# LoRA router: one exponential's row sum from ScalarE's accumulator output

## The chip, the cores and the metric

The kernel runs on one core of one Trainium2 chip. A time is the device time of one execution in microseconds (us). The kernel before took 86.59 us, the median of four runs that lie from 86.5 to 86.7.

## What is computed

A router gives each token a softmax over eight adapters. The reference is

```python
batch, seq, dim = 16, 512, 1024
num_loras = 8
# x: (16, 512, 1024) float32, router_weights: (1024, 8) float32

logits = np.matmul(x, router_weights)
exp_logits = np.exp(logits - np.max(logits, axis=-1, keepdims=True))
return (exp_logits / np.sum(exp_logits, axis=-1, keepdims=True)).astype(np.float32)
```

There are 8192 tokens of 1024 numbers: 32 MiB of x are read, and 8192 x 8 probabilities (256 KB) are written.

## The kernel before

**Tiling.** Token number p * 64 + j lies on partition p in row j, so each of the 128 partitions holds 64 rows (J = 64) of 1024 numbers. Each row j (128 tokens, one per partition) is one unit of work. TensorE transposes its eight 128x128 pieces (KO = 8); five land in the PSUM tile ptv and three in pts. VectorE copies ptv to xTv (L403), ScalarE copies pts to xTs (L355), and TensorE multiplies the eight pieces with the weights w_bf into eight logits per token, in the PSUM tile lg (L269 in the loop, L261 behind it). The loop of TensorE also multiplies a filler tile that is used for nothing.

**Softmax in groups.** For eight rows at a time (G = 8) VectorE takes the row maxima (L423, tile mx) and the differences (L423, tile ex), ScalarE the exponentials (L344, tile ev), and VectorE the sums (L439, ssum), the reciprocals (L443, inv) and the scaling into out_all (L423). These are spread between the copies of later rows.

**The end.** The last four rows (ALONE = 4) are not part of a group. For each, `low_alone(k)` takes the negated row maximum on VectorE (L454, tile low), and `power_alone(k)` the exponential on ScalarE with that maximum as bias (L348), from PSUM into row k of ev3. The last of all, row 63, arrives in three pieces; its transposes are at L315, their copies at L385 (ScalarE) and L460 (VectorE), its multiplication at L329. Then VectorE scales the last group (L423, `scale()`), sums the four rows of ev3 into sum3 (L507), takes four reciprocals into inv3 (L509) and multiplies (L511). In the profile ev and ev3 are both called ev, sum3 is called sum, and inv and inv3 are both called inv.

**Transfers.** GpSimd issues the loads of x with a cast to bf16 (L174, and L187 for the three pieces of row 63); the first four rows come from SyncE's queue. SyncE stores the result in two transfers: all rows but the last twelve (L165), and the last twelve (L167) when scaling and final product are both done.

**Order.** No scheduler moves anything: each engine's instructions stand in the order in which the code writes them, and engines wait for each other by semaphores that are written out. The ones that matter here are s_low (a row maximum is ready, VectorE to ScalarE), s_e3 (an exponential of the last four rows is ready, ScalarE to VectorE and TensorE), s_d (VectorE for itself, between dependent steps) and s_out (rows of the result are ready, VectorE to SyncE). A wait is written in two ways. `dve.wait_ge(s, n)` in front of an instruction is built into that instruction. `dve.wait_ge(s, n).then_inc(s, -n)`, which also counts the semaphore down, is built as an instruction of its own that stands in front; in the loop the waits ahead of L423 (row maxima), L439 and L344 are of this second kind, behind the loop they are of the first.

## Time and profile before

| what | value |
|---|---|
| median of four runs | 86.59 us (86.5 to 86.7) |
| the profiled execution | 86.53 us |
| its span, first to last instruction | 85.1 us |
| granted clock of TensorE, mean | 0.989 |
| HBM read | 33.59 MB, 398 GB/s over the span |
| TensorE busy (matmul) | 62.9 us, 74% |
| VectorE busy | 39.5 us, 46% |
| ScalarE busy | 38.0 us, 45% |
| one L348 exponential (128x8, bias from a tile) | 267 to 274 ns |
| the sum L507, reciprocal L509, product L511 | 186, 179, 192 ns |
| last store (48 KB), issue to landing | 1.5 us |

The table of busy time gives averages over the whole span. The order of the last operations is read from the timeline and from the chain of work that ended last, whose times are in microseconds from the span's start. An operation's row shows when it ran and not its wait; what ended the idle time in front of it stands in brackets behind it, as `[0.20 <-ACT ev L348]`. A name with a q, such as DVEq, is the engine's own sequencer: the engine was idle until its instruction stream got on.

### The profile page before, as it was taken

How to read it: one execution, taken by the hardware profiler on the slowest of the kernel's cores; microseconds unless marked ns; L12 is line 12 of the kernel's file. 1: busy time of each engine (PE TensorE's matmuls, PEld its weight loads, DVE VectorE, ACT ScalarE, POOL GpSimd, SP SyncE). 2: the span in 40 equal slices, each digit the busy share in tenths (PEclk: the TensorE clock that was granted, in tenths of full speed). 3: DMA queues.
4: the chain of work that ended last, by engine and by line, in shares of the span. 5: the costliest groups of instructions: out<-in, count | busy, mean ns of one | idle time of the engine just before them, and what ended most of it. 6: DMA issues, size and time to landing. Idle time of an engine off the chain costs nothing. (4 is left out here: it accounts for less than half of the span.)

```text
span 85.1 us, 2942 instructions
## 1 busy us (share of the span) xinstructions
PE 62.9 (74%) x1094; PEld 51.6 (61%) x1094; DVE 39.5 (46%) x114; ACT 38.0 (45%) x81; POOL 13.5 (16%) x30
## 2 busy tenths in 40 slices
PE   0054859999595977949596895949597799999860
PEld 0042748878484765828474673837476588777650
DVE  0020412685364442835266362736347257665662
ACT  0039683565254352535245262525336246545470
POOL 0489999800000000000000000000000000000000
PEclk9999999999999999999999999999999999999995
DMA  2999999999999999999999999999999999999920
GB/s 58 358 424 308 220 193 235 196 235 196 235 196 235 196 235 196 235 196 235 196 235 196 235 196 235 196 235 196 231 200 206 214 216 212 203 211 205 190 104 23
DMA packets 3904, 18.12 MB, mean 213 GB/s; under 512 B 568, under 2 KB 1080, under 8 KB 2112
## 3 DMA queue, kind: packets, MB, share of 16 engines
q0 software_dynamic: 3312, 15.73, 90.5%
q1 hardware_dynamic: 576, 2.36, 7.2%
q10 hardware_dynamic: 16, 0.03, 0.2%
HBM read 33.59 MB, written 0.26 MB: 398 GB/s over the span
## 5 line engine op out<-in xcount | busy, mean ns | idle before, releaser
L355 ACT COPY xTs<-pts 128x384 bf16<-128x384 bf16 x63 | 30.0, 477 | 37.4 <-PE pts L282 37.0
L403 DVE COPY xTv<-ptv 128x640 bf16<-128x640 bf16 x63 | 30.9, 491 | 32.9 <-PE ptv L282 30.4
L282 PE MATMUL ptv<-identity,x_all 128*128 128x128 bf16 x311 | 28.4, 223 | 13.6 <-PEq L218 12.3
L282 PEld LDWEIGHTS ptv<-identity,x_all 128*128 (+1 forms) x311 | 18.6, 98 | 15.0 <-issue 14.9
L282 PE MATMUL pts<-identity,x_all 128*128 128x128 bf16 x186 | 21.1, 224 | 0.0
L269 PEld LDWEIGHTS lg<-w_bf,xTv 128*128 128x128 bf16 x305 | 15.5, 98 | 7.4 <-issue 0.5
L269 PE MATMUL spare<-filler 128*128 128x512 bf16 x61 | 19.0, 393 | 0.5
L269 PE MATMUL lg<-w_bf,xTv 128*128 128x8 bf16 x305 | 16.6, 167 | 0.0
L282 PEld LDWEIGHTS pts<-identity,x_all 128*128 x186 | 13.5, 100 | 0.0
L269 PE MATMUL lg<-w_bf,xTs 128*128 128x8 bf16 x183 | 13.2, 166 | 0.0
L174 POOL DMA_DIRECT2D x_all<-in_x_dram x20 | 10.8, 605 | 2.8 <-POOLq L151 2.8
L269 PEld LDWEIGHTS lg<-w_bf,xTs 128*128 128x128 bf16 x183 | 8.9, 96 | 0.0
L269 PEld LDWEIGHTS spare<-filler 128*128 128x128 bf16 x61 | 4.3, 99 | 2.5 <-issue 2.5
L276 PE MATMUL lg<-ident,w 8*128 8x8 f32 x8 | 1.0, 250 | 5.3 <-PEq L274 5.3
L276 PEld LDWEIGHTS lg<-ident,w 8*128 8x128 f32 x8 | 0.9, 197 | 5.3 <-issue 5.3
L341 ACT CAST x_all<-x_f 128x1024 bf16<-128x1024 f32 x4 | 4.0, 1044 | 0.0
L423 DVE TENSOR_REDUCE mx<-lg 128x8 f32 x8 | 1.8, 224 | 4.4 <-DVEq L473 3.9
L341 ACT ACT_TABLE_LOAD x1 | 1.3, 1283 | 5.5 <-ACTq L339 5.5
L392 DVE CAST identity<-ident 128x128 bf16<-128x128 f32 x1 | 0.5, 516 | 5.3 <-POOL ident L180 5.3
L344 ACT ACTIVATE ev<-ex 128x64 f32<-128x64 f32 x8 | 2.1, 256 | 1.6 <-DVE ex L423 0.9
L439 DVE TENSOR_REDUCE ssum<-ev 128x8 f32<-128x64 f32 x8 | 1.8, 221 | 0.0
L187 POOL DMA_DIRECT2D x_all<-in_x_dram x3 | 1.7, 690 | 0.0
(41 smaller groups left out, 16.0 us busy)
## 6 DMA issues: line engine op xcount, KB each, us to landing
x_all<-in_x_dram POOLq DMA_DIRECT2D x12, 1024.0 KB, 32.1
x_f<-in_x_dram SPq DMA_DIRECT2D x2, 1024.0 KB, 6.3
x_all<-in_x_dram POOLq DMA_DIRECT2D x3, 512.0 KB, 59.9
x_all<-in_x_dram POOLq DMA_DIRECT2D x5, 256.0 KB, 64.1
out_dram<-out_all SPq DMA_DIRECT2D x1, 208.0 KB, 1.9
x_all<-in_x_dram POOLq DMA_DIRECT2D x1, 128.0 KB, 65.6
x_all<-in_x_dram POOLq DMA_DIRECT2D x2, 64.0 KB, 65.4
out_dram<-out_all SPq DMA_DIRECT2D x1, 48.0 KB, 1.5
```

Source lines behind the costliest of these rows:

```text
L174: nc.gpsimd.dma_start(out=xa[:, first[i]:first[i] + r, :], in_=x_rows[:, first[i]:first[i] + r, :]).then_inc(s_ld[i], 16)
L187: nc.gpsimd.dma_start(out=xa[:, J - 1, c], in_=x_rows[:, J - 1, c]).then_inc(s_z[i], 16)
L269: return pe.matmul(spare, lhsT=filler[:, 0:P], rhs=filler, start=True, stop=True)
L276: t = pe.transpose(w_ps[:, n, :], w8[:, :, n], ident[0:KO, 0:KO])
L282: turn_like = pe.transpose(turn_ap(0, 0), xa[:, 0, 0:P], identity).ins
L341: act.copy(xa[:, k, :], x_f32[:, k, :]).then_inc(s_cast, 1)
L344: return act.activation(ev, ex, func=Exp).then_inc(s_ev, 1)
L355: act.copy(xTs[j % 2], pts[j % 2][:, 0:SN, :]).then_inc(s_c[j % 2], 1)
L392: dve.tensor_copy(out=identity, in_=ident).then_inc(s_idb, 1)
L403: dve.tensor_copy(out=xTv[j % 2], in_=ptv[j % 2][:, 0:VN, :]).then_inc(s_c[j % 2], 1)
L423: return dve.add_instruction(kind(name=f"I-{nc.next_id()}", engine=dve.engine, **k))
L439: dve.reduce_sum(ssum[:, :, 0], ev, axis=X).then_inc(s_d, 1)
```

## The change

The exponential of the last row (k = 3) gets an accumulator output: ScalarE adds up the row's eight exponentials itself and writes the sum into sum3[:, 3]. VectorE's sum takes only the three rows ahead of it, waits for three exponentials instead of four, and stands ahead of the scaling of the last group instead of behind it. The reciprocal waits for that sum, and for the fourth exponential with its accumulator output.

```diff
     def power_alone(k):
         act.wait_ge(s_low, k + 1)
         act.activation(
-            ev3[:, k, :], alone[k], func=Exp, bias=low[:, k:k + 1]
+            ev3[:, k, :], alone[k], func=Exp, bias=low[:, k:k + 1],
+            accum_out=sum3[:, k, :] if k == ALONE - 1 else None,
         ).then_inc(s_e3, 1)
...
     low_alone(2)
     low_alone(3)
+    dve.wait_ge(s_e3, ALONE - 1)
+    dve.reduce_sum(sum3[:, 0:ALONE - 1, 0], ev3[:, 0:ALONE - 1, :], axis=X).then_inc(s_d, 1)
     scale()
+    dve.wait_ge(s_d, 4)
     dve.wait_ge(s_e3, ALONE)
-    dve.reduce_sum(sum3[:, :, 0], ev3, axis=X).then_inc(s_d, 1)
-    dve.wait_ge(s_d, 4)
     dve.reciprocal(inv3, sum3).then_inc(s_d, 1)
     dve.wait_ge(s_d, 5)
     dve.tensor_tensor(
```

In the built program the fourth exponential is followed by one more ScalarE instruction, without an input tensor, which writes sum3[:, 3] and increments s_e3. VectorE has as many operations as before, and one wait instruction more, on s_e3, in front of the reciprocal; the reciprocal itself carries the wait on s_d.

## The prediction

> **What bounds the kernel now.** I read three views, in this order: the table of busy tenths, the chain of work that ended last, and the timeline of the last microseconds.

> The busy table (40 slices of 2.13 us; digits are tenths) says what kind of end this is.

> ```profile
> DVE  0020412685364442835266362736347257665662
> ACT  0039683565254352535245262525336246545470
> DMA  2999999999999999999999999999999999999920
> ```

> The DMA engines are full (9) from the second slice to the 38th, so up to about 81 us the kernel waits for x. A change to two instructions per engine behind the last load cannot move that part. What follows the last load is serial, and every nanosecond there is a nanosecond of the kernel. The chain of work that ended last, in order of time (start us, length us, what), gives that tail:

> ```profile
> 81.93 0.38 PE lg L329 x8
> 82.31 0.02 issue
> 82.34 0.18 DVE low L454
> 82.52 0.02 issue
> 82.54 0.28 ACT ev L348
> 82.81 0.02 issue
> 82.84 0.20 DVE sum L507
> 83.04 0.02 issue
> 83.06 0.19 DVE inv L509
> 83.25 0.02 issue
> 83.27 0.19 DVE out_all L511
> ```

> The reader is to see five small operations in a row on two engines, each handing over in about 0.02 us. The step that the change aims at is the sum at L507: from the last exponential's end, 82.81, to the reciprocal's start, 83.06, is **0.25 us**. Behind the reciprocal nothing changes: product, store issued at 83.49, span end 85.1. So the whole question is how long 82.81 to the reciprocal lasts afterwards.

> **Part 1, the sum of three rows (moved ahead of the scaling).** It needs the third exponential. The timeline (start us, length us, engine, line, operation, and in brackets what ended the idle time before it) shows exponentials three and four as one entry:

> ```profile
> 82.14 0.66 ACT L348 ACTIVATE ev<-lg,low 128x8 f32<-128x8 f32 x2 [0.19 <-DVE low L454]
> 82.34 0.17 DVE L454 TENSOR_REDUCE low<-lg 128x1 f32<-128x8 f32 x1 [0.23 <-PE lg L329]
> 82.42 0.21 DVE L423 TENSOR_TENSOR out_all<-ev,inv 128x64 f32 x1
> ```

> At 268 ns each the third ends at 82.41 and is seen 0.03 later, at 82.44. VectorE could take its next instruction then: the scaling started at 82.42 behind the last row maximum (start 82.34). The sum's length lies between L454's 167 ns (8 elements) and L507's 186 ns (32); I take 0.18, so it ends at 82.62. Start-to-start distances of short VectorE instructions that wait for nothing new are 0.08 to 0.14 (82.34 to 82.42; 79.99 to 80.13), so the scaling starts at 82.52 to 82.58 and, at 215 ns, ends by 82.80. All of that lies beside ScalarE's last exponential and what follows it: **cost 0**. The cover is the time until the reciprocal can start, computed below as 83.03: 0.23 us to spare. Were the third exponential later than that by more than this, each excess nanosecond would count. The last store waits for scaling and final product alike, and the scaling is still the earlier one by about 0.6 us; it issues no DMA itself. No other engine waits for it.

> **Part 2, the accumulator's output on ScalarE.** In the built program this is not a free flag: behind the last exponential stands one more ScalarE instruction that has no input tensor, writes the one sum per partition, and carries the increment of s_e3 that the exponential carried before. No row shows such a read. Lower bound 0: it stands behind the exponential in order and carries its signal, so it can't gain. Upper bound: a full exponential with pointer bias, L348's 268 ns, starting only when the first has ended, plus a 0.02 handover: 0.29. The nearest rows are ScalarE's fixed costs without a pointer. The copies take 477 ns for 384 elements (L355) and 586 ns for 512 (L385): 0.85 ns an element, which leaves 150 ns fixed. The exponential from SBUF (L344, 256 ns, 64 elements) leaves 256 - 54 = 202 ns. And ScalarE starts an instruction that waits for nothing about 0.10 us before the previous one ends: L344 runs from 79.70 to 79.96 and the copy behind it starts at 79.86; L385 runs from 81.20 to 81.79 and L348 starts at 81.68. So the read ends 0.05 to 0.10 us after the exponential; I take **+0.08**, as it is nearest to a small instruction without a pointer.

> **Part 3, the wait in front of the reciprocal.** Before, the sum carried the wait for s_e3 itself and the handover was 0.03 us (82.81 to 82.84). Now the reciprocal has two waits, s_d and s_e3. In the built program an instruction carries one; the reciprocal carries s_d, long satisfied, and **s_e3, the late one, becomes a wait instruction of its own** in front of it. The trace prices exactly this, because the same sum at L439 appears in both forms: in the loop its wait for the exponentials also counts the semaphore down and stands alone; behind the loop it doesn't and is carried. The timeline of the loop's sixth pass, and then that of the tail, with the same columns:

> ```profile
> 64.21 0.26 ACT L344 ACTIVATE ev<-ex 128x64 f32<-128x64 f32 x1
> 64.61 0.22 DVE L439 TENSOR_REDUCE ssum<-ev 128x8 f32<-128x64 f32 x1
> ```

> ```profile
> 79.70 0.26 ACT L344 ACTIVATE ev<-ex 128x64 f32<-128x64 f32 x1 [0.86 <-DVE ex L423]
> ...
> 79.99 0.22 DVE L439 TENSOR_REDUCE ssum<-ev 128x8 f32<-128x64 f32 x1
> ```

> At 256 ns the exponentials end at 64.47 and 79.96; the sum starts 0.14 us later with the separate wait and 0.03 us later with the carried one. VectorE's copy ended at 64.60, but as short instructions start 0.05 to 0.09 before the previous one ends, it did not hold the sum. The row maximum at L423 says the same: 0.15 us behind the last matmul in the loop (63.13 to 63.28), 0.04 in the tail (79.15 to 79.19); so does L344 itself, 0.13 behind its input in the loop (64.08 to 64.21), 0.04 in the tail (79.66 to 79.70). So the handover becomes **0.14 instead of 0.03**. Bounds: 0.03, if the wait costs as little as a carried one, and 0.15, the longest of these rows. Queued behind the waiting instruction are the reciprocal, the product and, on SyncE, the last store: the whole rest of the kernel.

> [...]

> **The sum.** Removed: 0.25 (82.81 to 83.06). Put in its place: 0.08 for the read and 0.14 for the handover, 0.22. Reciprocal at 82.81 + 0.22 = 83.03 instead of 83.06: **-0.03 us**. The profiled execution took 86.53 (span 85.1 and 1.43 around it), so 86.50 against it. The median of the four runs, 86.59, is 0.06 above that execution; on its level the forecast is **86.56 us**.

> **The rivals.**

> 1. *The separate wait is as cheap as a carried one.* Then 0.08 + 0.03 replaces 0.25: -0.14; with a free read too -0.22. On the median's level 86.45 to 86.37. For it: the tail's carried handovers of 0.02 to 0.03. Against: all three pairs above show +0.09 to +0.11, and the wait sits at the one place where its semaphore is last.

> 2. *Slower: the accumulator's read does not overlap.* Its input is the finished sum of the exponential in front, so it may have to start where that ends, 82.81. Then 0.02 + 0.15 to 0.27 stands in place of 0.08, and the total is 0.31 to 0.43 against 0.25: +0.06 to +0.18, on the median's level 86.65 to 86.77. For it: it is the only ScalarE pair in the kernel in which the second needs what the first leaves inside the engine. Against: the 0.10 us overlap of neighbours that share nothing, if their order is kept inside the engine. It decides from a read that ends 0.11 us behind the exponential: beyond that the kernel is slower.

> 3. *The tail does not set the time.* If the store's landing (1.5 us for the last 48 KB) had a grain coarser than a tenth, nothing would be seen: 86.59. The chain gives no sign of it.

> **How the numbers follow.** Faster or slower here means by over 0.2%, 0.17 us, about what a measurement of this kernel can tell from no change (the four runs lie from 86.5 to 86.7). Forecast (-0.06 to -0.01): 0.72, rival 1: 0.10, rival 2: 0.14, rival 3: 0.04. The bound of 0.17 cuts rival 1 in the middle: 0.05 of its 0.10; scatter of the medians adds 0.03: faster 0.08. Rival 2 reaches the bound only at its dear end, and with scatter in its favour: I give 0.10 of its 0.14, and 0.04 for scatter on the forecast: slower 0.14. That leaves 0.78 for no difference. The likeliest case alone, with the runs' scatter of 0.1, spans 86.46 to 86.66; the range takes in most of both rivals and runs from 86.40 to 86.74.

> **What the changed profile would show.** The three-row sum starts at about 82.44 and is followed by the scaling, both over by 82.8. ScalarE has a short row behind the last exponential, 150 to 200 ns long, beginning before that exponential ends. The reciprocal is named as waiting on VectorE's own sequencer, starts 0.14 us after that row's end, at about 83.03, and the store is issued at about 83.46. I am wrong in part 2 if the read ends over 0.11 us behind the exponential, wrong in part 3 if the reciprocal follows within 0.05 us of the read, and wrong in part 1 if the scaling ends after the read. The forecast falls with any of these that moves the reciprocal by over 0.17 us.

## The result and the profile after

The changed kernel took **86.71 us**, the median of 44 runs, against 86.58 for 67 runs of the kernel before; the ratio is 1.0015, with a 95% interval from 1.0011 to 1.0020. That is 0.10 to 0.17 us slower, where the prediction had 0.03 us less. The prediction was wrong in its sign, though the time lies inside its range and inside the 0.2% that it called no difference.

The tail itself did what was forecast. The chain that ended last, of the changed kernel (start us, length us, what):

```profile
82.40 0.18 DVE low L455
82.58 0.02 issue
82.60 0.37 ACT ev L348 x2
82.97 0.03 issue
83.00 0.02 DVEq L510
83.02 0.05 issue
83.07 0.19 DVE inv L511
83.26 0.03 issue
83.28 0.19 DVE out_all L513
```

The exponential and the accumulator's read are one entry of two instructions. Behind it stands an entry that the chain of before did not have, DVEq L510: VectorE's sequencer with the separate wait for s_e3. From the last row maximum's start to the reciprocal's start it is 82.40 to 83.07, 0.67 us; before it was 82.34 to 83.06, 0.72. The timeline of the changed kernel gives the single operations (start us, length us, engine, line, operation):

```profile
82.51 0.18 DVE L507 TENSOR_REDUCE sum<-ev 128x3 f32<-128x24 f32 x1
82.60 0.22 DVE L424 TENSOR_TENSOR out_all<-ev,inv 128x64 f32 x1
82.77 0.19 ACT L348 ACTIVATION_READ_ACCUMULATOR ev<-lg,low 128x1 f32 x1
83.07 0.18 DVE L511 RECIPROCAL inv<-sum 128x4 f32<-128x4 f32 x1 [0.25 <-ACT ev L348]
...
83.50 0.34 SPq L167 DMA_DIRECT2D out_dram<-out_all  x1
```

The three-row sum and the scaling are over at 82.82, a quarter of a microsecond ahead of the reciprocal. The read begins 0.10 us before its exponential ends (82.60 + 0.27 = 82.87) and is over at 82.96. The transfers are as before; in the busy table they end in the same slice:

```profile
DVE  0021413267574452735266362726347257656671
ACT  0039683355554352535245253524426246545580
DMA  3899999999999999999999999999999999999930
```

So the loss is not in these rows. It shows when a run's time is set against its span. Both profiled executions have a span of 85.077 us to the nanosecond, and yet the one of before took 86.53 and the one of after 86.66. Over the 46 runs of the changed kernel for which a span is given, the time outside the span is 1.63 us on average; over the 76 runs of the kernel before in the first three rounds of experiments it is 1.45 to 1.47 (the average of each round). The span itself averages 85.09 over those 46 runs and 85.14 over the 76. Spans are given to a tenth, and averages of them are good to a few hundredths. **Outside the span: +0.17. Inside: -0.05. Sum: +0.12**, the measured difference of the medians being 0.13. The -0.05 compares runs of different rounds, so it is weak by itself; the change at the lengths of before, further down, gives it again within one round.

### The profile page after: what moved, and what is told of

It is laid out like the page before. It is cut to its first block, busy times and chain, and to the rows that moved or that the text cites. A ratio compares the mean times of both kernels' runs of the same rounds, so it can differ in the third digit from the quotient of the medians.

```text
span 85.1 us, 2944 instructions
## 1 busy us (share of the span) xinstructions
PE 63.8 (75%) x1094; PEld 52.2 (61%) x1094; DVE 39.3 (46%) x114; ACT 38.0 (45%) x82; POOL 13.4 (16%) x30
## 5 line engine op out<-in xcount | busy, mean ns | idle before, releaser
L269 PE MATMUL spare<-filler 128*128 128x512 bf16 x61 | 19.5, 401 | 0.5
L344 ACT ACTIVATE ev<-ex 128x64 f32<-128x64 f32 x8 | 2.1, 256 | 1.5 <-DVE ex L424 0.9
```

Source lines behind the costliest of these rows:

```text
L269: return pe.matmul(spare, lhsT=filler[:, 0:P], rhs=filler, start=True, stop=True)
L344: return act.activation(ev, ex, func=Exp).then_inc(s_ev, 1)
```

## What could be behind it

Two theories were put against each other in the first runs.

**Theory A.** The tail gains what it seems to gain, and the time outside the span has grown because the programs of ScalarE and VectorE are one instruction longer each: 65 instructions instead of 64 on ScalarE (the accumulator's read) and 70 instead of 69 on VectorE (the separate wait). Something at the start or at the end of an execution goes by these lengths.

**Theory B.** The loss lies in the tail: the read and the separate wait cost more in the timed runs than the one profile shows.

Below, "64/69" stands for 64 instructions in ScalarE's built program and 69 in VectorE's. The lengths are changed by the idle semaphore increments at the start of both programs, which nobody waits for; the kernel before has 11 on ScalarE and 5 on VectorE (`DVE_IDLE, ACT_IDLE = 5, 11`).

## Experiments

Times are medians, and ratios are against runs of the kernel before on the same chip.

### One instruction more behind ScalarE's program

```diff
     for k in range(1, ALONE):
         power_alone(k)
+    act.sem_inc(s_idle, 1)
```

> The kernel before with one semaphore increment, which nobody waits for, behind the last instruction of ScalarE's program (65 instructions instead of 64); the tail's operations are untouched. Theory A (the loss of the change lies outside the tail, in a ScalarE program that is one instruction longer): +0.10 to +0.18 us against before. Theory B (the loss lies in the tail's read and wait): 0.00, within 0.04.

Measured: **87.24 us** against 86.61, ratio 1.0068 (1.0054 to 1.0081). The span was 85.16 on average, that of before in the same round 85.15; the time outside it was 2.05 against 1.45. One instruction that does nothing costs 0.6 us, and all of it outside the span. Theory A has the sign and the place; its size, taken from the changed kernel, is far too small here.

### One instruction more behind VectorE's program

```diff
     ).then_inc(s_out, 1)
+    dve.sem_inc(s_idle, 1)
```

> The kernel before with one semaphore increment, which nobody waits for, behind the last instruction of VectorE's program (70 instructions instead of 69). Theory A, if it is the length of ScalarE's program: 0.00; if any engine's length counts: +0.05 to +0.18. Theory B: 0.00, within 0.04.

Measured: 86.70 us against 86.61, ratio 1.0010 (1.0001 to 1.0019); outside the span 1.58. So VectorE's length counts too; the time by itself barely shows it, the time outside the span does (1.58 against 1.45).

### The change with the two waits in the other order

```diff
-    dve.wait_ge(s_d, 4)
     dve.wait_ge(s_e3, ALONE)
+    dve.wait_ge(s_d, 4)
     dve.reciprocal(inv3, sum3).then_inc(s_d, 1)
```

In the built programs of the change and of this kernel the reciprocal carries the wait that is written first, and the second stands in front of it as an instruction of its own: in the chain of the change it is the entry DVEq L510. So here the reciprocal carries s_e3, and s_d, long satisfied, stands alone.

> The changed kernel with the reciprocal's two waits written in the other order, so that the reciprocal carries the late one (s_e3) and the early one (s_d) stands alone. Both theories: the handover from the accumulator's read to the reciprocal falls from 0.11 to 0.02-0.04 us, the time by 0.07 to 0.09 against the changed kernel. Theory A: +0.04 to +0.06 against before. Theory B: -0.10 to -0.14 against before.

Measured: 86.64 us against 86.61, ratio 1.0009 (0.9994 to 1.0024), a result that doesn't tell it from before; outside the span 1.61, span 85.06 against 85.15. The trace has the read's end at 82.999 and the reciprocal's start at 83.031, and no DVEq entry in the chain: the handover is 0.03 us, and with the late wait apart it was 0.11. Theory A had +0.04 to +0.06 for the time; the median is 0.03 above before and the mean, which one long run of 87.26 raises, 0.06. Theory B's -0.10 to -0.14 lies outside the interval.

### The change with ScalarE's program back at 64

```diff
-    DVE_IDLE, ACT_IDLE = 5, 11
+    DVE_IDLE, ACT_IDLE = 5, 10
```

> The changed kernel with one of the eleven idle semaphore increments at ScalarE's start left out, so that its program has 64 instructions again; everything else stands one instruction earlier. Theory A: -0.13 to -0.20 against the changed kernel, -0.07 to 0.00 against before. Theory B: as the changed kernel, +0.13 against before.

Measured: 86.59 us against 86.61, ratio 0.9992 (0.9981 to 1.0003). Outside the span 1.52 on average, but spread from under 1.3 to 1.7, more than any other kernel. It points to theory A, and alone it would be inconclusive.

### The change at the lengths of before

```diff
-    DVE_IDLE, ACT_IDLE = 5, 11
+    DVE_IDLE, ACT_IDLE = 4, 10
```

> The changed kernel with one idle semaphore increment fewer at the start of ScalarE's and of VectorE's program, so that these have 64 and 69 instructions as before. Theory A (the program's length adds time outside the span): the time outside the span is 1.45 as before, no instruction-fetch packet behind the last instruction, span -0.05, so 86.53 to 86.58 against 86.60 before: -0.03 to -0.08. Theory B (the tail is longer): +0.13 against before.

Measured: **86.52 us** against 86.58, ratio 0.9991 (0.9982 to 1.0000). Outside the span 1.47, as before; span 85.08 against 85.13. In the trace the reciprocal starts 0.665 us behind the last row maximum, the changed kernel's 0.67. This is the change without the lengths: mean time and span are both 0.05 below before, and the interval of the time just reaches no change.

### The same with the swapped waits

The edit is that of the last two experiments together: the order of the waits, and 4 and 10 idle increments.

> The same, and the reciprocal carries the wait for s_e3 while s_d stands alone. Theory A: span -0.13 against before, outside 1.45, so -0.10 to -0.15 against before. Theory B: 0.00 to +0.05 against before.

Measured: 86.49 us against 86.58, ratio 0.9991 (0.9982 to 1.0000); mean 86.49 against 86.60. Outside the span 1.48, span 85.01 against 85.13. Its chain:

```profile
82.34 0.18 DVE low L455
82.52 0.02 issue
82.54 0.37 ACT ev L348 x2
82.91 0.02 issue
82.93 0.19 DVE inv L511
```

There is no DVEq entry any more: 82.34 to 82.93 is 0.59 us, 0.13 less than before and 0.08 less than with the separate wait. The span follows (-0.12); in the time the two kernels with and without the separate wait lie 0.03 to 0.06 apart, less than the 0.08, and their intervals overlap. Against before the time is 0.09 (medians) to 0.10 (means) less, where theory A expected 0.10 to 0.15.

### The tail of before at the lengths of the change

```diff
-    DVE_IDLE, ACT_IDLE = 5, 11
+    DVE_IDLE, ACT_IDLE = 6, 12
```

> The kernel before with one idle semaphore increment more at the start of ScalarE's and of VectorE's program, so that these have 65 and 70 instructions as in the changed kernel, and the tail of before. Theory A: outside the span 1.60 to 1.65, span as before or up to 0.02 longer, so +0.14 to +0.22 against before. Theory B: 0.00 to +0.03.

Measured: **86.78 us** against 86.58, ratio 1.0021 (1.0012 to 1.0030). Outside the span 1.67 against 1.47, span 85.11 against 85.13. The chain is that of before, five operations and the same distances:

```profile
82.36 0.18 DVE low L454
82.53 0.02 issue
82.56 0.28 ACT ev L348
82.83 0.02 issue
82.86 0.20 DVE sum L507
83.05 0.02 issue
83.08 0.19 DVE inv L509
```

82.36 to 83.08 is 0.72, as before. The kernel has no accumulator output, no separate wait on the path and no reordering, and it loses more than the changed kernel did. This and the change at the lengths of before are the pair that decides: the change at 64/69 does not lose (0.9991, 0.9982 to 1.0000), the old tail at 65/70 does (1.0021, 1.0012 to 1.0030). Theory B falls.

### The reordering alone

The edit is shown against the changed kernel. One idle increment of VectorE is left out as well (`DVE_IDLE, ACT_IDLE = 4, 11`), so that the lengths are 64/69.

```diff
-            accum_out=sum3[:, k, :] if k == ALONE - 1 else None,
...
     scale()
-    dve.wait_ge(s_d, 4)
     dve.wait_ge(s_e3, ALONE)
+    dve.reduce_sum(sum3[:, ALONE - 1:ALONE, 0], ev3[:, ALONE - 1:ALONE, :], axis=X).then_inc(s_d, 1)
+    dve.wait_ge(s_d, 5)
     dve.reciprocal(inv3, sum3).then_inc(s_d, 1)
-    dve.wait_ge(s_d, 5)
+    dve.wait_ge(s_d, 6)
```

> No accumulator: VectorE sums three rows ahead of the scaling as in the change, and the last row's eight exponentials in a sum of its own that carries the wait for s_e3 (one idle increment left out, 64 and 69 instructions). This is the change's reordering alone. In the tail the last sum has 8 elements (0.16 us) instead of 32 (0.19), so both theories: -0.02 to -0.03 in the span, -0.05 to 0.02 in the time; a loss would mean that the reordering itself costs.

Measured: 86.59 us against 86.58, ratio 1.0000 (0.9991 to 1.0009). In its chain the last sum is the shorter one:

```profile
82.43 0.18 DVE low L454
82.61 0.02 issue
82.63 0.28 ACT ev L348
82.91 0.02 issue
82.93 0.17 DVE sum L509
83.11 0.02 issue
83.13 0.19 DVE inv L511
```

82.43 to 83.13 is 0.70 instead of 0.72. Moving three rows ahead costs nothing and shortens the chain by 0.02, which neither the time nor the average span (85.13, as before) shows.

### 65 and 69: the place of the instruction, or the length

The next kernel is that of before with `DVE_IDLE, ACT_IDLE = 5, 12`.

> The kernel before with one idle increment more at the start of ScalarE's program: 65 and 69 instructions, as with the trailing increment that took 0.6 us, but the extra one stands at the front. If the lengths 65 and 69 make the loss: outside the span about 2.05, +0.60 against before. If the place behind the last operation makes it: outside 1.55 to 1.65, +0.10 to +0.20. If ScalarE's length does not matter: 0.00. The span stays in all of them.

Measured: 87.11 us against 86.59, ratio 1.0063 (1.0047 to 1.0079); outside the span 2.01. The extra instruction costs nearly as much at the front (0.55 in the mean) as behind the end (0.60). It is the length that counts, and not the place.

The kernel after that has the accumulator's read and nothing else of the change:

```diff
-            ev3[:, k, :], alone[k], func=Exp, bias=low[:, k:k + 1]
+            ev3[:, k, :], alone[k], func=Exp, bias=low[:, k:k + 1],
+            accum_out=unused if k == ALONE - 1 else None,
```

> The kernel before with the accumulator output added to the last exponential, written to a tile that nobody reads; VectorE sums all four rows as before and carries the wait for s_e3. It prices the accumulator's read alone: the handover from the exponential's end to VectorE's sum grows from 0.03 to 0.12-0.13 us, +0.09 in the span. Its programs have 65 and 69 instructions, the last of ScalarE's being the read: by the lengths the time outside the span is as in the kernel with one more increment at the front, by the trailing increment's place it is 1.55 to 1.65. So +0.20 to +0.30, or +0.65 to +0.75, against before.

Measured: 87.35 us against 86.59, ratio 1.0082 (1.0069 to 1.0096); outside the span 2.06, span 85.28 against 85.14. Its chain prices the read:

```profile
82.57 0.18 DVE low L456
82.75 0.02 issue
82.77 0.37 ACT ev L349 x2
83.14 0.02 issue
83.16 0.20 DVE sum L509
```

The sum starts 0.59 us behind the row maximum, where it was 0.50 before (82.34 to 82.84). The read's row is 193 ns long, and 0.09 of it lie behind the exponential. The rest of the loss, 0.6, is that of the lengths 65/69 for the third time, now with a different sort of instruction.

### Shorter programs

The kernel before with `DVE_IDLE, ACT_IDLE = 5, 10`:

> The kernel before with one idle increment fewer at the start of ScalarE's program: 63 and 69 instructions. If time outside the span grows only above 64 and 69: 1.45 to 1.48 outside, 0.00 against before. If 64 is only one good length among others: outside 1.55 or more, +0.10 or more.

Measured: 86.58 us against 86.59, ratio 0.9998 (0.9989 to 1.0007); outside the span 1.48. One instruction fewer on ScalarE alone gives nothing.

The swapped waits with 63/68 (`DVE_IDLE, ACT_IDLE = 3, 9`):

> The change with the swapped waits and two idle increments fewer in each program: 63 and 68 instructions. If only more than 64 and 69 costs: as with 64 and 69 instructions, -0.08 to -0.13 against before, no fetch packet behind the last instruction. If shorter is better still: outside below 1.45 and -0.15 or more.

Measured: **86.27 us** against 86.59, ratio 0.9966 (0.9953 to 0.9979); outside the span 1.36, span 84.98 against 85.14. It beats both kernels. Its chain has the short tail, 82.51 to 83.10, 0.59 us:

```profile
82.51 0.18 DVE low L455
82.69 0.02 issue
82.71 0.37 ACT ev L348 x2
83.08 0.02 issue
83.10 0.19 DVE inv L511
```

The tail of before with 63/68 (`DVE_IDLE, ACT_IDLE = 4, 10`):

> The kernel before with one idle increment fewer in each of ScalarE's and VectorE's programs: 63 and 68 instructions, tail of before. If the time outside the span goes by the lengths alone, whatever the tail: outside 1.36 as in the swapped kernel of these lengths, span as before, so -0.08 to -0.12 against before. If the gain of that kernel outside the span came from its tail: 1.45 outside, 0.00.

Measured: 86.58 us against 86.71 on that chip, ratio 0.9985 (0.9977 to 0.9994); outside the span 1.34 against 1.47, span 85.25 against 85.24. Tail and lengths act each for itself: -0.10 (mean time) to -0.13 (chain) for the swapped tail and -0.13 for the lengths, -0.25 for both in the mean of the five runs of the kernel above.

### Further lengths

The kernel before with `DVE_IDLE, ACT_IDLE = 5, 13`, 66/69:

> The kernel before with two idle increments more in ScalarE's program: 66 and 69 instructions. If every instruction above 64 adds: outside above 2.05, over +0.6 against before. If it is one step at 65: outside 2.00 to 2.06, +0.55 to +0.6. If 65 with 69 is a single bad pair of lengths: outside below 1.7, +0.00 to +0.25.

Measured: 87.22 us against 86.71, ratio 1.0064 (1.0051 to 1.0076); outside the span 1.98. With 69 on VectorE, 65 is a step, not a single bad length: 66 costs no more than 65.

The kernel before with an instruction more on SyncE:

```diff
     sp.wait_ge(s_z[0], 16)
+    sp.sem_inc(s_idle, 1)
+    sp.sem_inc(s_idle, 1)
```

(In the built program the first increment goes into the wait's instruction and the second is one of its own: 49 instructions instead of 48.)

> The kernel before with one instruction more in SyncE's program (49 instead of 48), a semaphore increment ahead of its first store that nobody waits for; ScalarE and VectorE keep 64 and 69. If the time outside the span goes by any engine's length: outside 1.55 or more, +0.10 or more. If by ScalarE's and VectorE's alone: 1.45 to 1.48 outside, -0.02 to +0.03.

Measured: 86.71 us against 86.71, ratio 1.0006 (0.9997 to 1.0015); outside the span 1.45 against 1.47. SyncE's length by one does nothing here.

### The lengths side by side

| ScalarE/VectorE | kernels | outside the span | instruction packet behind the span |
|---|---|---|---|
| 63/68 | swapped waits; before | 1.36; 1.34 | none |
| 63/69 | before | 1.48 | none |
| 64/69 | before; the change; swapped waits; reordering alone; SyncE one more | 1.45 to 1.47; 1.47; 1.48; 1.47; 1.45 | none |
| 64/70 | before and one behind VectorE; the change | 1.58; 1.52 | 86.45; 86.39 |
| 65/70 | the change as it was made; swapped waits; before | 1.63; 1.61; 1.67 | 86.49; 86.47; 86.48 |
| 65/69 | before, one more at the front; one behind the end; unused accumulator output | 2.01; 2.05; 2.06 | 86.89; 87.02; 87.19 |
| 66/69 | before | 1.98 | 87.08 |

The reader is to see two things. Within a row the time outside the span is the same to a few hundredths, whatever the tail does and wherever the extra instruction stands (the kernel with 64/70 and a wide spread is the loosest). And the packet behind the last instruction is in the trace of each of the nine kernels with more than 64 or more than 69 instructions, and of none of the others; 1.39 to 1.42 us behind the span's end with 70 on VectorE, 1.79 to 1.82 with 65 or 66 on ScalarE and 69 on VectorE.

The packet can be set against the time of the same execution. Three of the nine, in us from the span's start:

| kernel | packet's start | its length | its end | time of this execution | end minus time |
|---|---|---|---|---|---|
| the change as it was made, 65/70 | 86.49 | 0.42 | 86.91 | 86.66 | 0.25 |
| before, one behind the end, 65/69 | 87.02 | 0.49 | 87.51 | 87.27 | 0.24 |
| before, 66/69 | 87.08 | 0.31 | 87.39 | 87.14 | 0.25 |

In all nine the last column lies between 0.235 and 0.247, while the packet's length goes from 0.31 to 0.53 and time minus the packet's start from 0.06 to 0.29. So in these kernels the time follows the packet's end, to a hundredth of a microsecond: the packet is not mere company. What the constant 0.24 is, the traces do not show, because they do not show where a run's time begins.

**What stays open.** That the lengths make the loss is shown by edits to nothing else. That the run's end waits for the instruction packet is read from nine traces and not shown by an edit: no run takes the packet away at the same length. Why these lengths bring the packet, why it starts 0.4 us later with 65/69 than with 65/70, and why 63/68, without any packet, is 0.1 us better than 63/69, no run here tells. The lengths of TensorE's and GpSimd's programs were not changed. Nor do the traces show what an engine does outside the span.

## Why the prediction was wrong

**The bound and the chain** were right: the tail behind the last load sets the end of the span, and the chain after has the steps that were forecast: row maximum, exponential with its read, reciprocal and product, without the sum that stood between them before.

**Part 1, cost 0 for the three-row sum:** right. It started at 82.51, 0.11 behind the row maximum, where the forecast had 0.10, and scaling was over 0.25 us ahead of the reciprocal (0.23 forecast). The reordering alone lost nothing.

**Part 2, +0.08 for the read:** right. It is 0.09 (82.87 to 82.96 in the changed kernel; 0.50 to 0.59 with the unused output). The read overlaps with its exponential by 0.10 us, as its neighbours do, so rival 2 did not occur.

**Part 3, 0.14 instead of 0.03 for the handover:** right in kind, and a little too dear. It is 0.11 (82.96 to 83.07), and 0.03 when the reciprocal carries the late wait. The rows taken from the loop price it at 0.13 to 0.15; the tail has 0.11. The loop's waits also count their semaphore down, and the tail's does not; whether that is the difference, no run tells. The sign that the prediction named, the reciprocal waiting on VectorE's own sequencer, stands in the chain (DVEq L510), while the timeline's bracket names ScalarE's ev. In the chain the wait's entry is at 83.00 and 0.02 us long, and the reciprocal starts 0.05 us behind its end. A late wait that stands alone cost 0.08 us in two pairs of kernels: 0.11 against 0.03 for the handover at 65/70, 0.665 against 0.59 from row maximum to reciprocal at 64/69.

**The sum inside the span, -0.03:** measured -0.05 to -0.06.

**The step that failed** is the next one: "The profiled execution took 86.53 (span 85.1 and 1.43 around it), so 86.50 against it". It carried the 1.43 over unchanged. The prediction had both facts in hand that speak against this, one more instruction in ScalarE's built program and one more in VectorE's, and priced them only as operations in the tail. As a change of the programs' lengths they cost 0.17 us outside the span (1.63 against 1.45 to 1.47), three times what the tail gained. None of the three rivals covers it: rival 2 ended on the right side, but with another mechanism, and rival 3 doubted the span's end and not the time beyond it. The chance of 0.78 for a difference within 0.2% held in size only.

## What to carry to other kernels

When a change adds or removes instructions, the time outside the span can change (here it lay between 1.34 and 2.06 us), and is a term of its own: compare each run's time with its span before a difference of a tenth of a microsecond is explained from the chain. Test a small change at equal program lengths, by padding both versions with instructions that nobody waits for, and then try the lengths themselves: here 63/68 with the short tail took 0.3% off the kernel. Where an instruction has two waits, see in the built program which one it carries, and let that be the one that comes last: here the handover took 0.03 us so, and 0.11 us with the late wait apart.

## What the runs showed of the hardware that was not expected

An instruction that does nothing, at either end of ScalarE's program, cost 0.5 to 0.6 us of a run of 86.6 without moving the span (outside the span 2.01 and 2.05 against 1.45). One more on VectorE cost 0.1 (1.58 against 1.45); on top of 65 on ScalarE it took 0.4 us back (1.61 to 1.67 with 65/70, 2.01 to 2.06 with 65/69). With the longer programs the traces show an instruction packet behind the span, 1.39 to 1.82 us from its end, and a time 0.24 us short of that packet's end in all nine traces that have it.

In the changed kernel's trace the accumulator's read is an instruction of 193 ns for one number per partition, nearly the fixed cost of 202 ns that the prediction took from the exponential of 64 elements, and it begins 0.10 us before the exponential that it reads from ends.
